# Hybrid Conformer and differential-attention block on one core: the first norm's squares taken from the channel-major x

## The chip, the cores and the metric

The kernel runs on one core of one Trainium2 chip. The metric is the device time of one execution in microseconds (us); lower is better. PE is TensorE, the matrix engine; DVE, ACT and POOL are the vector, scalar and GpSimd engines; SP is SyncE, whose queue issues most transfers. "Group 0" below is the first pair of 256-column groups of the input projection, "group 1" the next 256 columns.

## The reference, cut to what matters

T = 256 tokens, D = 2048 channels, one layer, all in float32:

```python
h = rmsnorm(x, norm_mix_g)                       # x * rsqrt(mean(x^2) + 1e-6) * g
a, g, q, k, v = split(h @ w_in)                  # 2048 -> 1024+1024 | 1024 | 1024 | 1024
u = layernorm(causal_dwconv(a * sigmoid(g), width 31))
conv_out = silu(u)
attn_out = rmsnorm(diff_attention(q, k, v, lam)) * (1 - lambda_init)
x = x + concat(conv_out, attn_out) @ w_out
gate, up = split(rmsnorm(x, norm_ffn_g) @ w_up)  # 2048 -> 2 x 5632
x = x + (gelu(causal_dwconv(gate, width 3)) * up) @ w_down
return rmsnorm(x, norm_final_g)
```

## The kernel before

Every product is split: x and each weight are cut into a rounded part `hi` and a rest `lo`, and three products per 128 input channels (hi by x-hi, hi by x-lo, lo by x-hi) are summed in PSUM. ACT writes the weights' `hi` (`split`, L151), DVE subtracts to `lo` (L152); `hi` and `lo` have three buffers each, one holding 1024 columns. `split_rows` does the same for x times the norm's gain (ACT L113, DVE L114). The kernel has five stages: input projection with the first norm, attention and convolution woven in between groups, output projection, gated FFN, down projection with the final norm.

**Start.** x comes channel-major as `xt` and is read with the weights in pieces of one or two blocks of 128 channels (`XPARTS`). The first `SIDE` pieces of x are issued by ACT (L258), everything else by SP through `fetch` (L139), in the order in which the code is written; SP first issues the gain `mix_g`. `WARM` matmuls on a tile of ones (L240, two PE passes each) run ahead of the first product. Group 0 multiplies block by block as the pieces arrive (L283) into four PSUM tiles `first`: two for the 256 columns of `a`, two for the 256 columns of `g`. The pool `acc` has just these four buffers. The next 256 columns of `a` (`early`) are loaded behind it in pieces of 8, 4 and 4 blocks.

**First norm.** The factor 1/rms of each token (`rstd1`) is not multiplied into x but into the products. Its squares come from a token-major copy `x_sb`, four loads of 512 KB among those of `early`: ACT squares with a running sum (L295), DVE adds the four parts (L298), POOL raises to the power -1/2 (`rsqrt_of`, L95, L96), and `spread` makes a row of it: DVE scales an identity (L102), PE multiplies it by ones (L103), DVE copies the result out as `rb1` (L104).

**Turn from group 0 to group 1.** As soon as group 0 is summed, `first` is copied out of PSUM, which needs no `rb1`, and multiplied later:

```python
if j == 0:
    with prio(ATT):
        nc.scalar.copy(a_, pa[n])
nc.vector.tensor_tensor(a_, a_ if j == 0 else pa[n], rb1, op=ALU.mult)
```

(L374 and L375; the same for `g_` on DVE, L382 and L383.) `channel_group` (L208 to L210) then takes two of the `acc` buffers per 256 columns.

**Order.** SP, ACT and DVE each run their instructions in a fixed order. SP's is that of the code; that of ACT and DVE comes from a scheduler that sorts by priority (`prio`); PE's is by hand from the group loop on. Small steps of attention and LayerNorm sit in a list `bg`; every fourth block of a group runs one of them (`tick`). At the end of the input projection the list holds `seq(ln_total, ln_mean, turn), value, None, ln_var, put, ln_apply`: the LayerNorm's sum over channels (L555), its mean by a matmul (L560), differences and squares (L566 to L574), and the variance by `token_sums` (two 128x1 products L109, copy L110), `rsqrt_of` and `spread`.

**Tail.** The last 512 columns of the down projection end token half by token half; the second half is cut in two parts of 256 columns. Of the last part DVE adds the residual (L708), ACT squares it with a sum (L710), POOL adds the sum to the earlier ones and takes the power (L718, L719), then DVE and ACT scale four pieces of 512 columns (L724 to L728), each stored by SP (L729).

## Time and profile before

| what | value |
| --- | --- |
| median of three runs | 1089.92 us (1089.47 to 1090.38) |
| the profiled execution: own time, span | 1090.31 us, 1088.5 us |
| PE busy | 1077.5 us, 99% of the span |
| DVE busy, ACT busy, POOL busy | 764.9 us, 599.1 us, 15.3 us |
| moved by DMA | 205.89 MB, mean 189 GB/s |

The span lies 1.8 us inside the profiled execution's own time, and that time lies 0.39 us above the median. "Busy" counts instructions as the profile shows them. A row of the timeline gives the start, the length (of all the instructions on the row together), the engine, the source line, the operation with destination and source, and how many there are; in brackets stands how long the engine idled before and what ended the wait. Lengths of instructions on one engine overlap by some hundredths of a microsecond, so the pace is read from starts.

### The profile page before, as it was taken

Reading aid. Unit: us, or ns where it says so; the run is one execution under the profiler, and the core shown is the slowest. Engines: PE = TensorE matmul, PEld = TensorE weight load, DVE = VectorE, ACT = ScalarE, POOL = GpSimd, SP = SyncE. Lnnn points to the kernel's source line nnn. Section 1 sums busy time; section 2 is a strip of 40 time slices with the busy share of each in tenths; the row PEclk is TensorE's granted clock in tenths of the full one; section 3 lists DMA queues with packets and bytes.
Section 4 is the critical chain, followed back from the end, with each engine's and each line's share of the span. In section 5 each row is a group of like instructions: output and inputs, shape, how many; then the busy total and the mean of one; then the engine's idle time right before and its main releaser. Section 6 shows DMA issues by size and latency. Waiting matters only on the chain.

```text
span 1088.5 us, 16124 instructions
## 1 busy us (share of the span) xinstructions
PE 1077.5 (99%) x6311; PEld 951.5 (87%) x6311; DVE 764.9 (70%) x1202; ACT 599.1 (55%) x973; POOL 15.3 (1%) x44
## 2 busy tenths in 40 slices
PE   9999999999999999999999999999999999999996
PEld 9999999998888888888888888888888888888885
DVE  6799999988765777776777677776777445454544
ACT  6776889886755454545445444544545434343432
POOL 0000000001000000000000000000000000000000
PEclk9999999999999999999999999999999999999998
DMA  9755544444555555555555555555555655555553
GB/s 352 244 192 185 190 165 152 155 163 148 201 178 178 186 194 192 184 183 181 193 191 193 194 187 180 184 189 189 194 193 190 231 192 196 192 194 193 195 166 107
DMA packets 32844, 205.89 MB, mean 189 GB/s; under 512 B 3712, under 2 KB 4480, under 8 KB 9600
## 3 DMA queue, kind: packets, MB, share of 16 engines
q1 hardware_dynamic: 32336, 203.55, 54.2%
q8 instruction: 49, 0.80, 0.3%
q0 software_dynamic: 144, 1.05, 0.2%
q10 hardware_dynamic: 288, 0.26, 0.1%
q14 instruction: 27, 0.22, 0.1%
HBM read 202.75 MB, written 2.10 MB: 188 GB/s over the span
## 4 chain that ended last, share of the span: by engine, by line
PE 97%; DMA 1%; DVE 1%; ACT 0%; issue 0%; POOL 0%; POOLq 0%; DVEq 0%; SPq 0%; ACTq 0%
PE acc L187 30%; PE acc L190 15%; PE acc L218 11%; PE acc L220 11%; PE acc L219 11%; PE acc L208 5%; PE acc L210 5%; PE acc L209 5%; PE acc L283 2%; DMA v_sb<-in_w_in 1%; PE misc L629 0%; PE misc L426 0%; PE misc L423 0%; PE misc L454 0%; DVE lo L152 0%; ACT hi L151 0%
## 5 line engine op out<-in xcount | busy, mean ns | idle before, releaser
L152 DVE TENSOR_TENSOR lo<-raw,hi 128x1024 fp32r<-128x1024 f32 x368 | 450.0, 1223 | 270.0 <-ACT hi L151 268.7
L151 ACT CAST hi<-raw 128x1024 fp32r<-128x1024 f32 x368 | 386.6, 1051 | 389.3 <-PE acc L220 171.5
L187 PE MATMUL acc<-actT,hi 128*128 128x512 f32 x1408 | 481.7, 395 | 0.0
L190 PE MATMUL acc<-actT,lo 128*128 128x256 f32 x1408 | 368.8, 280 | 0.0
L187 PEld LDWEIGHTS acc<-actT,hi 128*128 128x128 f32 x1408 | 253.3, 188 | 48.5
L190 PEld LDWEIGHTS acc<-actT,lo 128*128 128x128 f32 x1408 | 265.4, 188 | 13.7
L219 PE MATMUL acc<-lo,fT 128*128 128x512 f32 (+1 forms) x355 | 137.5, 387 | 0.0
L220 PE MATMUL acc<-hi,fT 128*128 128x512 f32 (+1 forms) x355 | 137.5, 387 | 0.0
L208 PE MATMUL acc<-actT,hi 128*128 128x256 f32 x448 | 127.6, 285 | 0.0
L210 PE MATMUL acc<-actT,lo 128*128 128x256 f32 x448 | 127.0, 283 | 0.2 <-DVE lo L152 0.2
L209 PE MATMUL acc<-actT,hi 128*128 128x256 f32 x448 | 126.8, 283 | 0.0
L218 PE MATMUL acc<-hi,fT 128*128 128x512 f32 (+1 forms) x355 | 123.8, 387 | 0.0
L208 PEld LDWEIGHTS acc<-actT,hi 128*128 128x128 f32 x448 | 85.9, 192 | 0.7 <-issue 0.7
L210 PEld LDWEIGHTS acc<-actT,lo 128*128 128x128 f32 x448 | 85.9, 192 | 0.4 <-DVE lo L152 0.4
L209 PEld LDWEIGHTS acc<-actT,hi 128*128 128x128 f32 x448 | 85.9, 192 | 0.0
L220 PEld LDWEIGHTS acc<-hi,fT 128*128 128x128 f32 x355 | 66.7, 188 | 13.7
L219 PEld LDWEIGHTS acc<-lo,fT 128*128 128x128 f32 x355 | 66.7, 188 | 13.6
L218 PEld LDWEIGHTS acc<-hi,fT 128*128 128x128 f32 x355 | 66.7, 188 | 13.5
L345 ACT ACTIVATE tap<-u,cols 128x256 f32<-128x256 f32 x160 | 71.0, 503 | 3.7 <-DVE cv L346 2.0
L234 ACT COPY half<-acc 128x256 f32<-128x256 f32 x88 | 32.4, 368 | 56.9 <-PE acc L187 56.9
L346 DVE TENSOR_TENSOR cv<-cv,tap 128x512 f32<-128x512 f32 x80 | 54.7, 685 | 3.0 <-ACT tap L345 1.2
L219 PE MATMUL acc<-lo,mixT 128*128 128x512 f32 x128 | 50.2, 392 | 0.0
(180 smaller groups left out, 913.6 us busy)
## 6 DMA issues: line engine op xcount, KB each, us to landing
raw<-in_w_up SPq DMA_DIRECT2D x88, 1024.0 KB, 4.9
raw<-in_w_down SPq DMA_DIRECT2D x43, 1024.0 KB, 4.9
raw<-in_w_in SPq DMA_DIRECT2D x35, 1024.0 KB, 4.9
raw<-in_w_out SPq DMA_DIRECT2D x14, 1024.0 KB, 4.9
mixT<-in_w_in SPq DMA_DIRECT2D x4, 512.0 KB, 8.4
x_sb<-in_x SPq DMA_DIRECT2D x4, 512.0 KB, 11.0
raw<-in_w_out SPq DMA_DIRECT2D x4, 512.0 KB, 3.5
out<-x_sb SPq DMA_DIRECT2D x8, 256.0 KB, 2.9
```

The lines of the kernel that those rows point to most:

```text
L151: cast(hi, src)
L152: nc.vector.tensor_tensor(lo, src, hi.bitcast(F32), op=ALU.subtract)
L187: nc.tensor.matmul(ps[n], lhsT=hi[:, cs], rhs=xT[:, k], start=(k == 0), stop=last)
L190: nc.tensor.matmul(ps[n][:, 1, :], lhsT=lo[:, cs], rhs=xT[:, k, 0, :], start=False, stop=last)
L208: nc.tensor.matmul(ps[n], lhsT=hi[:, cs], rhs=xT[:, k, 0, :], start=(k == 0), stop=False)
L209: nc.tensor.matmul(ps[n], lhsT=hi[:, cs], rhs=xT[:, k, 1, :], start=False, stop=False)
L210: nc.tensor.matmul(ps[n], lhsT=lo[:, cs], rhs=xT[:, k, 0, :], start=False, stop=(k == KD - 1))
L218: nc.tensor.matmul(ps, lhsT=xT[:, k, 0, ts_], rhs=hi, start=(k == first), stop=False)
L219: nc.tensor.matmul(ps, lhsT=xT[:, k, 0, ts_], rhs=lo, start=False, stop=False)
L220: nc.tensor.matmul(ps, lhsT=xT[:, k, 1, ts_], rhs=hi, start=False, stop=(k == last))
L345: nc.scalar.activation(tmp[:, n, :], upad[c][:, k : k + T], AF.Copy, scale=cwcol(k, c))
L346: nc.vector.tensor_tensor(cv[j], cv[j], tmp, op=ALU.add)
```

## The change

Squares of the first norm are now taken from the channel-major pieces: ACT squares each piece (L272), DVE adds the squares up (L275, L294), and `token_sums` adds them over channels. The `x_sb` loads move into the loop over the query groups, one each; `early` is loaded in two pieces of 8 blocks with the parameters between them. ACT issues only piece 0 of x, and `mix_g` behind it; SP starts with the first weights. Four one-block pieces become six, ten warm-ups eight. Group 0's copies go: `rb1` is multiplied straight from PSUM (L372, L378). The list at the end of the input projection is `turn, seq(ln_total, ln_mean, value), None, None, seq(ln_var, put), ln_apply`. In the tail DVE squares with a running sum (`last_part`), POOL takes only the power, and the second token half is stored in five pieces of 256 to 512 columns over the queues of SP and ACT.

```diff
     AHEAD = -200
-    XPARTS = [1, 1, 1, 1, 2, 2, 2, 2, 2, 2]
-    WARM = 10
-    SIDE = 2
+    XPARTS = [1, 1, 1, 1, 1, 1, 2, 2, 2, 2, 2]
+    WARM = 8
+    SIDE = 1
     ATT = -300
     HALF = 1024
...
-        ss1 = const.tile([P, NT, D // XW], F32, name="ss1")
+        sq1 = p1.tile([P, 2, T], F32, name=f"cv{CC // GW - 1}")
...
                 nc.scalar.dma_start(xraw[:, k0 : k0 + nk, :], xt[:, k0 : k0 + nk, :])
+                nc.scalar.dma_start(mix_g, norm_mix)
             pieces.append((k0, nk, raw, spans))
...
-            if i == 0:
-                fetch(mix_g, norm_mix)
...
                 split_rows(xT[:, k, 0, :], xT[:, k, 1, :], xraw[:, k, :], mix_g[:, k : k + 1])
+            h0 = k0 % 2
+            sqs = p2.tile([P, 2, T], F32, name="tap") if i > 1 else sq1
+            sq = sqs[:, h0 : h0 + nk, :]
+            nc.scalar.activation(sq, xraw[:, k0 : k0 + nk, :], AF.Square)
+            if i > 1:
+                total = sq1[:, h0 : h0 + nk, :]
+                nc.vector.tensor_tensor(total, total, sq, op=ALU.add)
             cast = nc.vector.tensor_copy if i == 0 else nc.scalar.copy
...
-        early = load(wi, 0, 8, GW, GW)
-        for i in range(D // XW):
-            if i == 2:
-                early.extend(load(wi, 8, 4, GW, GW))
-            cs = slice(i * XW, (i + 1) * XW)
-            fetch(x_sb[:, :, cs], xv[:, :, cs])
-            for t in range(NT):
-                junk = misc.tile([P, 512], F32, name="misc")
-                nc.scalar.activation(junk, x_sb[:, t, cs], AF.Square, accum_out=ss1[:, t, i : i + 1])
-        early.extend(load(wi, 12, 4, GW, GW))
         with prio(ATT):
-            nc.vector.tensor_reduce(rstd1, ss1, axis=AX.X, op=ALU.add)
+            nc.vector.tensor_tensor(sq1[:, 0, :], sq1[:, 0, :], sq1[:, 1, :], op=ALU.add)
+            token_sums(rstd1, sq1[:, 0, :])
             rsqrt_of(rstd1, rstd1, D, NORM_EPS, NT)
             spread(rb1, rstd1)
+        early = load(wi, 0, 8, GW, GW)
         load_params()
+        early.extend(load(wi, 8, 8, GW, GW))
...
             for n in range(2):
                 a_ = p2.tile([P, T], F32, name=f"a{n}")
-                if j == 0:
-                    with prio(ATT):
-                        nc.scalar.copy(a_, pa[n])
-                nc.vector.tensor_tensor(a_, a_ if j == 0 else pa[n], rb1, op=ALU.mult)
+                with prio(ATT if j == 0 else 0):
+                    nc.vector.tensor_tensor(a_, pa[n], rb1, op=ALU.mult)
                 an.append(a_)
             pg = first[2:] if j == 0 else channel_group(wi, CC + j * GW, xT, n_conv=RATE_A)
             for n in range(2):
                 g_ = p2.tile([P, T], F32, name="g_")
-                if j == 0:
-                    with prio(ATT):
-                        nc.vector.tensor_copy(g_, pg[n])
-                nc.vector.tensor_tensor(g_, g_ if j == 0 else pg[n], rb1, op=ALU.mult)
+                with prio(ATT if j == 0 else 0):
+                    nc.vector.tensor_tensor(g_, pg[n], rb1, op=ALU.mult)
                 gn.append(g_)
             for n in range(2):
...
+            cs = slice(j * XW, (j + 1) * XW)
+            fetch(x_sb[:, :, cs], xv[:, :, cs])
             pq = channel_group(wi, 2 * CC + j * GW, xT, n_conv=RATE_Q)
...
-        bg.extend([seq(ln_total, ln_mean, turn), value, None, ln_var, put, ln_apply])
+        bg.extend([turn, seq(ln_total, ln_mean, value), None, None, seq(ln_var, put), ln_apply])
...
-        STORES = (("dve", 0, 512), ("act", 512, 1024), ("dve", 1024, 1536), ("dve", 1536, 2048))
+        STORES = {
+            0: ((nc.vector, nc.sync, 512), (nc.scalar, nc.sync, 512), (nc.vector, nc.sync, 512), (nc.vector, nc.sync, 512)),
+            1: (
+                (nc.vector, nc.sync, 256), (nc.scalar, nc.scalar, 384), (nc.vector, nc.sync, 512),
+                (nc.vector, nc.sync, 448), (nc.vector, nc.scalar, 448),
+            ),
+        }
...
-        def finish(t, ss):
+        def last_part(t, ps, cs, before):
+            xs = x_sb[:, t, cs]
+            nc.vector.tensor_tensor(xs, ps, xs, op=ALU.add)
+            sums = const.tile([P, 1], F32, name=f"sums{t}_{cs.start}")
+            junk = misc.tile([P, 512], F32, name="misc")
+            nc.vector.tensor_tensor_reduce(
+                out=junk[:, : cs.stop - cs.start], in0=xs, in1=xs, scale=1.0 / D, scalar=before,
+                op0=ALU.mult, op1=ALU.add, accum_out=sums,
+            )
+            return sums
+
+        def finish(t, sums, cs):
             r3 = rstd3[:, t : t + 1]
-            for part in ss:
-                nc.gpsimd.tensor_tensor(r3, part, r3, op=ALU.add)
-            nc.gpsimd.tensor_tensor(r3, r3, mhalf[:, 0:1], op=ALU.pow)
-            c0 = D - XW
-            for eng, lo_, hi_ in STORES:
...
+            nc.gpsimd.tensor_tensor(r3, sums, mhalf[:, 0:1], op=ALU.pow)
+            lo_ = 0
+            for eng, queue, width in STORES[t]:
+                xs = x_sb[:, t, lo_ : lo_ + width]
+                cut = min(max(cs.start - lo_, 0), width)
+                if cut < width:
+                    xg = xs[:, cut:]
+                    nc.vector.scalar_tensor_tensor(xg, xg, r3, gf[:, lo_ + cut : lo_ + width], op0=ALU.mult, op1=ALU.mult)
+                if not cut:
+                    pass
+                elif eng is nc.scalar:
+                    nc.scalar.activation(xs[:, :cut], xs[:, :cut], AF.Copy, scale=r3)
                 else:
-                    nc.vector.tensor_scalar_mul(xs, xs, r3)
-                nc.sync.dma_start(ov[:, t, lo_:hi_], xs)
+                    nc.vector.tensor_scalar_mul(xs[:, :cut], xs[:, :cut], r3)
+                queue.dma_start(ov[:, t, lo_ : lo_ + width], xs)
+                lo_ += width
...
+            whole = slice(c0, D)
+            finish(0, last_part(0, pd[0], whole, rstd3[:, 0:1]), whole)
...
-            ss4 = const.tile([P, 2], F32, name="ss4")
...
-            residual(1, pd[1][:, left], slice(c0, c0 + hw), ss4[:, 0:1])
+            sums = last_part(1, pd[1][:, left], slice(c0, c0 + hw), rstd3[:, 1:2])
...
+            xl = x_sb[:, 1, c0 : c0 + hw]
...
-            residual(1, tail, slice(c0 + hw, D), ss4[:, 1:2])
-            finish(1, [ss4[:, 0:1], ss4[:, 1:2]])
+            sums = last_part(1, tail, slice(c0 + hw, D), sums)
+            nc.vector.tensor_tensor(xl, xl, gf[:, c0 : c0 + hw], op=ALU.mult)
+            finish(1, sums, slice(c0 + hw, D))
```

PE's order at the turn from group 0 to group 1, before (L283 is group 0, L208 to L210 group 1, L103 the `spread` of `rb1`):

```order
L283 MATMUL acc<-actT,hi 128x256 x2
L283 MATMUL acc<-actT,lo 128x256
L208 MATMUL acc<-actT,hi 128x256 [waits Activation_49]
L209 MATMUL acc<-actT,hi 128x256
L210 MATMUL acc<-actT,lo 128x256 [waits DVE_49]
```

and with the change (L289 is group 0 now, L109 the sums over channels, `cv_105` the buffer of squares):

```order
L289 MATMUL acc<-actT,hi 128x256 x2
L289 MATMUL acc<-actT,lo 128x256
L109 MATMUL misc<-ones,cv_105 128x1 [waits DVE_49]
L109 MATMUL misc<-ones,cv_105 128x1
L103 MATMUL misc<-diag,ones 128x128 [waits DVE_49] x2
L208 MATMUL acc<-actT,hi 128x256 [waits DVE_49,Activation_49]
L209 MATMUL acc<-actT,hi 128x256
```

The sums and `spread` moved from inside group 1 to a place between the groups, and the first product of group 1 waits for DVE as well as ACT.

DVE's order at the same place with the change (`raw`, `hi` and `lo` are the early weights, `nlam` the attention's lambda):

```order
L152 TENSOR_TENSOR lo<-raw,hi 128x1024 [waits PE_49,Activation_49]
L309 TENSOR_TENSOR nlam<-ls 128x1 [waits Activation_49]
L110 COPY rstd_104<-misc 128x2 [waits PE_49]
L310 TENSOR_SCALAR nlam<-nlam 128x1 [waits DVE_49]
L152 TENSOR_TENSOR lo<-raw,hi 128x1024 [waits DMAHW2_49,Activation_49]
L102 TENSOR_SCALAR diag<-ident,rstd_104 128x128 [waits Pool_49]
L102 TENSOR_SCALAR diag<-ident,rstd_104 128x128
L314 TENSOR_SCALAR nrq_482<-rstd_104 128x2
L104 COPY rb_106<-misc 128x256 [waits PE_49]
L372 TENSOR_TENSOR a_502<-acc,rb_106 128x256 [waits DVE_49]
L372 TENSOR_TENSOR a_504<-acc,rb_106 128x256
```

The third `lo` of the early weights stands between the copy of the sums (L110) and the scaled identity (L102), and the multiplication out of PSUM (L372) stands where the copies used to be.

ACT's order at the start, with the change (L258 and L259 are its transfers of piece 0 and `mix_g`, L272 the squares of pieces 0 and 1, L113 the split of x):

```order
L258 DMA mixT<-in_xt 128x256
L259 DMA mix_g<-in_norm_mix 128x16
L262 ACT_TABLE_LOAD
L262 ACTIVATE touch<-mhalf 128x8 [waits Pool_49]
L272 ACTIVATE cv_105<-mixT 128x256 [waits DMAHW0_49]
L272 ACTIVATE cv_105<-mixT 128x256 [waits DMAHW2_49]
L113 ACTIVATE actT<-mixT,mix_g 128x256 [waits DMAHW3_49]
L113 ACTIVATE actT<-mixT,mix_g 128x256
```

Both squares stand ahead of the first split of x, and the second waits for piece 1 of x; before, the split was ACT's first work on x.

## Rows read from the trace of the kernel before

**Rows 1.** Page part 1, the whole span: engine, busy us, share, instructions.

```profile
PE 1077.5 (99%) x6311; PEld 951.5 (87%) x6311; DVE 764.9 (70%) x1202; ACT 599.1 (55%) x973; POOL 15.3 (1%) x44
```

**Rows 2.** Page part 4, the chain that ended last: share by engine.

```profile
PE 97%; DMA 1%; DVE 1%; ACT 0%; issue 0%; POOL 0%; POOLq 0%; DVEq 0%; SPq 0%; ACTq 0%
```

**Rows 3.** Timeline of PE, 0 to 15 us (columns as described above).

```profile
0.98 4.64 PE L240 MATMUL misc<-ones 128*128 128x128 f32 x20 [0.98 <-POOL ones L86]
5.27 2.01 PE L283 MATMUL acc<-actT,hi 128*128 128x256 f32 x8
...
7.59 1.12 PE L283 MATMUL acc<-actT,hi 128*128 128x256 f32 x8
...
12.23 1.22 PE L283 MATMUL acc<-actT,hi 128*128 128x256 f32 x8 [0.17 <-ACT hi L151]
...
14.06 1.12 PE L283 MATMUL acc<-actT,hi 128*128 128x256 f32 x8
```

**Rows 4.** Windows: us, busy PE PEld DVE ACT POOL, granted clock, DMA share, GB/s.

```profile
5.00:7.00 2.00, 2.00 (x11) 2.00 (x11) 1.84 (x4) 1.56 (x4) 0.00 (x0) 1.00 1.03 363
...
40.00:50.00 10.00, 9.76 (x81) 9.55 (x81) 9.90 (x18) 7.32 (x12) 0.00 (x0) 1.00 0.54 173
```

**Rows 5.** Timeline of SP's queue, DVE and ACT, 1 to 5 us.

```profile
1.17 0.90 SPq L139 DMA_DIRECT2D v_sb<-in_w_in  x2
...
4.46 0.43 DVE L151 CAST hi<-v_sb 128x512 fp32r<-128x512 f32 x1 [0.39 <-DMA v_sb<-in_w_in]
...
4.71 0.51 ACT L113 ACTIVATE actT<-mixT,mix_g 128x256 fp32r<-128x256 f32 x1 [1.14 <-DMA mixT<-in_xt]
```

**Rows 6.** Timeline of DVE, 16 to 19 us, in group 0.

```profile
16.13 1.22 DVE L152 TENSOR_TENSOR lo<-mixT,hi 128x1024 fp32r<-128x1024 f32 x1
...
18.08 1.22 DVE L152 TENSOR_TENSOR lo<-mixT,hi 128x1024 fp32r<-128x1024 f32 x1
```

**Rows 7.** Timeline of ACT and PE at the turn, 28.9 to 31 us.

```profile
28.93 0.62 ACT L374 COPY a<-acc 128x256 f32<-128x256 f32 x2
...
29.91 0.28 PE L208 MATMUL acc<-actT,hi 128*128 128x256 f32 x1
...
30.69 1.04 ACT L151 CAST hi<-raw 128x1024 fp32r<-128x1024 f32 x1
```

**Rows 8.** Timeline of PE and DVE, 38.7 to 42.6 us, in group 1.

```profile
38.78 0.61 PE L103 MATMUL misc<-diag,ones 128*128 128x128 f32 x4
...
39.43 0.42 DVE L104 COPY rb<-misc 128x256 f32<-128x256 f32 x1 [1.58 <-PE misc L103]
...
39.89 0.76 DVE L375 TENSOR_TENSOR a<-a,rb 128x256 f32<-128x256 f32 x2
...
42.51 0.39 PE L210 MATMUL acc<-actT,lo 128*128 128x256 f32 x1 [0.24 <-DVE lo L152]
```

**Rows 9.** Timeline of PE, DVE and POOL, 255 to 269 us, the LayerNorm.

```profile
255.13 0.70 PE L560 MATMUL misc<-part,onesc 128*128 128x256 f32 x2 [0.69 <-DVE part L555]
...
263.01 0.43 DVE L574 TENSOR_TENSOR part<-u 128x256 f32<-128x256 f32 x1
...
265.89 0.50 PE L109 MATMUL misc<-ones,part 128*128 128x1 f32 x4
...
266.95 0.70 POOL L96 TENSOR_TENSOR rln<-rln,mhalf 128x2 f32<-128x2 f32 x1
...
268.31 0.47 DVE L102 TENSOR_SCALAR diag<-ident,rln 128x128 f32<-128x128 f32 x2
```

**Rows 10.** Timeline of DVE, ACT and POOL, 1080 to 1082.2 us, the tail.

```profile
1080.21 0.42 DVE L708 TENSOR_TENSOR x_sb<-acc,x_sb 128x256 f32<-128x256 f32 x1
...
1080.67 0.39 ACT L710 ACTIVATE misc<-x_sb 128x256 f32<-128x256 f32 x1 [0.35 <-DVE x_sb L708]
...
1081.59 0.55 POOL L719 TENSOR_TENSOR rstd<-rstd,mhalf 128x1 f32<-128x1 f32 x1
```

**Rows 11.** Page part 6, transfers: count, KB each, median us from issue to landing.

```profile
out<-x_sb SPq DMA_DIRECT2D x8, 256.0 KB, 2.9
```

More of the change, by code (lines that the diff above doesn't have):

```diff
@@ L713, in residual @@
             )
-        def finish(t, ss):
-            r3 = rstd3[:, t : t + 1]
-            for part in ss:
-                nc.gpsimd.tensor_tensor(r3, part, r3, op=ALU.add)
-            nc.gpsimd.tensor_tensor(r3, r3, mhalf[:, 0:1], op=ALU.pow)
-            c0 = D - XW
-            for eng, lo_, hi_ in STORES:
-                xs = x_sb[:, t, lo_:hi_]
-                if hi_ == D:
-                    nc.vector.scalar_tensor_tensor(xs, xs, r3, gf[:, c0:], op0=ALU.mult, op1=ALU.mult)
-                elif eng == "act":
-                    nc.scalar.activation(xs, xs, AF.Copy, scale=r3)
-                else:
-                    nc.vector.tensor_scalar_mul(xs, xs, r3)
-                nc.sync.dma_start(ov[:, t, lo_:hi_], xs)
+        def last_part(t, ps, cs, before):
[9 more added lines that the diff above has]
+        def finish(t, sums, cs):
+            r3 = rstd3[:, t : t + 1]
+            nc.gpsimd.tensor_tensor(r3, sums, mhalf[:, 0:1], op=ALU.pow)
[10 more added lines that the diff above has]
+                    nc.scalar.activation(xs[:, :cut], xs[:, :cut], AF.Copy, scale=r3)
+                else:
+                    nc.vector.tensor_scalar_mul(xs[:, :cut], xs[:, :cut], r3)
+                queue.dma_start(ov[:, t, lo_ : lo_ + width], xs)
+                lo_ += width
         def plain_end(s, pd):
@@ L754, in block_kernel @@
             token_step(pd[0], rest, 0, fT, 0, NF - 1)
-            residual(0, pd[0], slice(c0, D), ss3[:, 0, s : s + 1])
-            finish(0, [ss3[:, 0, s : s + 1]])
+            whole = slice(c0, D)
+            finish(0, last_part(0, pd[0], whole, rstd3[:, 0:1]), whole)
             token_step(pd[1], rest[:-CUT], 1, fT, 0, NF - 1)
-            ss4 = const.tile([P, 2], F32, name="ss4")
             hw = XW // 2
```

## The prediction, made before the changed kernel had run

> **What bounds the kernel now.** I read the shares of busy time first, then the chain of waits, then the timelines of the places that the change touches. PE is busy for 1077.5 of 1088.5 us [rows 1] and holds 97% of the chain that ended last [rows 2]; DVE at 70% and ACT at 55% stand beside it. So a microsecond counts only if PE loses or regains it, or if it lies behind PE's last product. The reader is to see in the timelines where PE is not at its pace. At the start its products come at half of it: the first eight of group 0 take 2.01 us, the next eight hi products 1.12 [rows 3]. In group 0 it waits for pieces of weights near 12 us, in group 1 once for DVE's `lo` at 42.5 us [rows 8], and before the LayerNorm's mean for DVE's sum [rows 9]. Everything else between 7 and 1079 us runs at one product of 256 columns per 0.12 us. The change has about 2 us of such waits to win, and some 3 us at the tail to shorten a little.
>
> All sums are made on the profiled execution, own time 1090.31 us, 0.39 above the median of 1089.92.
>
> **First product, +0.2 (-0.1 to +0.7).** Today it starts at 5.27, when the 20 passes of the warm-ups, (5.27 - 0.98) / 20 = 0.2145 each, are done [rows 3]. Sixteen passes end at 0.98 + 16 x 0.2145 = 4.41. But ACT's new order has the squares of pieces 0 and 1 ahead of the first split of x, and piece 1 is now SP's second transfer. Today it is ACT's second, and ACT takes it up at 4.71 [rows 5]. On SP it stands one issue slot of 0.45 us (0.90 for two, [rows 5]) behind the weights, which leave one slot earlier than today, so I expect it near 4.5. Then comes a square of 128x256 (0.39 in the tail's row [rows 10]; with the step to the next 0.45) and the split, 0.51 [rows 5]: about 5.5. Early end: piece 1 at 4.2, so 5.2. Late end: piece 1 at 4.7 and full lengths, some 5.7, and 6.0 if `mix_g`, now behind x on ACT's queue, is late too. The eight slow products stay slow in either case.
>
> **Waits for pieces in group 0, -0.7 (-0.7 to 0).** Blocks 1 to 3 take 3 x 1.44 us from 7.59, so block 4 could start at 11.91; it starts at 12.23, and its twelve products last until 14.06 where 1.44 would do [rows 3]: 0.32 + 0.39 lost, while ACT casts a piece of two blocks that came whole. With six single blocks the cast of block 4 takes half as long and waits for half the bytes, so the loss should go. It stays if the transfers are late for another reason. The squares are new work in group 0, per two blocks one square and one DVE sum of 128x512. DVE's pace today is 18.08 - 16.13 = 1.95 us per two blocks [rows 6]; with some 0.7 for the sum it is 2.65, under PE's 2.88. Cost there: nothing, with 0.2 us of cover.
>
> **Turn from group 0 to group 1, +3.85 (+3.2 to +4.4).** Today ACT copies the `a` sums out at 28.93 and group 1 starts at 29.91 with no gap [rows 7]; the norm's chain runs beside group 1, `spread` interrupts PE at 38.78 for four passes of 0.11, 0.45 in all [rows 8]. Now the four PSUM buffers come free only by the multiplication by `rb1`, and the whole chain lies between the groups on PE's own queue. Let T be the end of group 0:
> - Sums over channels, copy and power: in the LayerNorm the same steps run from 265.89 to 266.95 + 0.70 = 267.65, so T + 1.76 [rows 9].
> - DVE cannot scale the identity then. The third early `lo` stands ahead of it and needs ACT's cast of a buffer that group 0's last products free: the cast takes 1.04 [rows 7], the `lo` 1.22 [rows 6], so DVE is at it until T + 2.35.
> - One scaled identity, 0.47 / 2 [rows 9]: T + 2.6.
> - PE's matmul to DVE's copy, 39.43 - 38.78 = 0.65; the copy to the multiplication, 39.89 - 39.43 = 0.46; one multiplication, 0.42 [rows 8]: T + 4.13. With the step to PE group 1 starts at T + 4.2, and its first products run some 0.1 slower, as after the wait at 42.5.
>
> That is 4.3, less the 0.45 which `spread` costs today: 3.85. If the scheduler's `lo` were out of the way, the chain alone gives 1.76 + 0.25 + 0.65 + 0.46 + 0.42 + 0.1, less 0.45: 3.2. If ACT's cast is half a microsecond late, 4.4. The copies that go were hidden and bring nothing. The weights of group 1 are there (SP has no `x_sb` ahead of them), so nothing else is late behind it.
>
> The rule that speaks against this edit is in the Trainium skill, Perfetto Trace Analysis, Matmuls: independent matmul groups should rotate through PSUM banks, so that one's evacuation overlaps the next one's products. By that rule kept, as today, the term would be about -0.45 and the sum -1.6; by the new order the rotation is gone.
>
> **Wait at 42.5 us, -0.4 (-0.5 to 0).** PE idles until DVE's `lo` arrives, behind the four multiplications at 39.89 [rows 8]. They move to the turn, so this goes unless DVE's backlog only shifts.
>
> **LayerNorm's order, -0.25 (-0.85 to +0.3).** `turn` ahead of `ln_mean` gives DVE time for its sum; the wait at 255.13 (0.69 idle, 0.85 with the slower restart) goes [rows 9]. In return mean and variance are two empty steps apart plus `value`, three steps in all. The chain between them ran from 255.13 to 263.01 + 0.43, 8.3 us [rows 9]; beside one more `lo` and cast it is 10.5. The three steps from the mean to the sums take 265.89 - 255.13 = 10.8 today [rows 9], less what `value` brought, some 10. About 0.6 of new wait is the middle, and none or 1.15 the ends.
>
> **x_sb in the query groups, 0.** Four loads of 512 KB go to stretches in which DMA is about half busy (0.54, [rows 4]). They cost an issue slot of 0.45 each on SP ahead of weights that are loaded two buffers early. If that cover is gone, 512 KB at the 363 GB/s of [rows 4] is 1.4 us once, part of the upper end of the last term.
>
> **Tail, -0.2 (-0.6 to +0.3).** From ACT's square at 1080.67 to the power at 1081.59 lie 0.92 us [rows 10]. DVE's square with sum lasts about as long as the residual's 0.42 [rows 10], with the step to POOL 0.55: the power starts 0.35 earlier. But the end is a stream of 1 MB; one store takes 2.9 us to land [rows 11], and narrower pieces on two queues shift only when it begins. I take half.
>
> **DVE without slack, +0.2 (0 to +0.8).** From 40 to 50 us DVE is busy 9.90 of 10 [rows 4]. PE and DVE both stand still at the turn, and what DVE defers (taps, `lo`) it has no room to make up there; one wait like that at 42.5 may come back.
>
> Sum: 0.2 - 0.7 + 3.85 - 0.4 - 0.25 - 0.2 + 0.2 = +2.7. 1090.31 + 2.7 = 1093.0, less 0.39: **1092.6 us**. The ends that go together leave 1091 to 1093.8 for this case alone.
>
> **The rivals.**
> - **A, the clock.** There are now a hole of 1 us between warm-ups and products and one of 4.2 us at the turn. The granted clock prints 1.00 for 5 to 7 us [rows 4], but the products there come every 0.213 us, 256 columns at 1.2 GHz, and after 7.1 us every 0.12; before that PE had been working since 0.98 [rows 3]. If PE comes back at the lower level after a hole and keeps it as long as at the start, 6.1 us, it loses 0.44 of each: 2.7. For it: the holes are longer than any that PE has today once it is up. Against it: after the wait at 42.5 only one product was slow. In the middle 1.9, so 1094.5 (1093.4 to 1095.3). The Trainium skill says, in TensorE: Matmul & The Clock Gate, Part 1, that "the default state is throttled, and activity releases the throttle"; no stretch of this trace shows a fall.
> - **B, the other side: group 1 is not held by `rb1`.** If its first products find a free buffer, or the chain is done by T because the sums run ahead of the last blocks, the term of 3.85 is about 0, and 1088.7 is left; with the first product at 4.5 and no new LayerNorm wait 1087.2. It decides where T + 4.2 falls below T. Against it: PE's written order has the sums behind group 0's last product and the wait for DVE on group 1's first.
> - **C, the first product comes early.** If piece 1 lands by 3.5, the warm-ups' end at 4.41 is the limit, 0.95 better than the forecast: 1091.7. For it: nothing but `mix_g` and x are ahead of the weights now. Against it: ACT could take piece 1 up at 4.71 today [rows 5].
>
> **How the numbers follow.** A measurement of this kernel tells about 0.2%, 2.2 us, from no change: slower begins at 1092.1, faster at 1087.7. The forecast has 0.62: 0.40 above 1092.1, 0.21 within, 0.01 faster. A has 0.18, all slower. B has 0.10: 0.06 the same, 0.04 faster. C has 0.10: 0.08 the same, 0.02 slower. That makes 0.60 slower, 0.35 the same, 0.05 faster. The range of 1090.6 to 1095.2 takes in the forecast but for its far ends, C and nearly all of A, and leaves B out.
>
> **What would show it.** PE's timeline should have a hole of about 4 us between L289 and L208, broken by L109 and L103, with L372 as what ends it; no wait near 12 and 42 us; a first product near 5.5 behind ACT's split; a short wait ahead of the LayerNorm's L109 and none ahead of L560. The forecast is wrong if group 1 starts within 1 us of group 0's end, if the hole is over 5 us, if products of 0.21 us follow it, or if DVE's lost time returns as waits over 1 us before 100 us.

## The result, and the profile after

| | median | range | runs | profiled execution: own time, span |
| --- | --- | --- | --- | --- |
| before | 1089.84 us | 1089.47 to 1090.38 | 6 | 1090.31, 1088.5 us |
| changed | 1096.66 us | 1095.79 to 1097.08 | 6 | 1095.86, 1093.8 us |

The ratio is 1.0062, with a 95% interval of 1.0051 to 1.0073: 6.8 us slower. That is the forecast's side but past its range (up to 1095.2). The changed kernel's executions spread over 1.3 us, and the profiled one lies 0.8 below their median. One execution of a later kernel (e9) took 2171.16 us, twice as long as all others, and is left out of every figure here.

The shares of the whole span hardly moved (page parts 1 and 4; against [rows 1, 2]):

```profile
PE 1079.0 (99%) x6311; PEld 952.8 (87%) x6311; DVE 772.1 (71%) x1220; ACT 596.7 (55%) x961; POOL 15.3 (1%) x41
```

```profile
PE 96%; DVE 2%; issue 1%; ACT 1%; DMA 0%; POOLq 0%; POOL 0%; DVEq 0%; ACTq 0%
```

The places are found in the timelines again. PE at the start (columns as before: start, length, engine, line, what, how many, wait):

```profile
0.98 3.78 PE L240 MATMUL misc<-ones 128*128 128x128 f32 x16 [0.98 <-POOL ones L86]
6.10 1.26 PE L289 MATMUL acc<-actT,hi 128*128 128x256 f32 x8 [1.34 <-ACT actT L113]
...
7.68 1.12 PE L289 MATMUL acc<-actT,hi 128*128 128x256 f32 x8
```

The first product comes at 6.10, behind 1.34 us of idle PE, but its eight take 1.26 and not 2.01 [rows 3]: the clock was up already. Block 1 begins at 7.68 against 7.59, there is no wait near 12 us, and group 0's last product begins at 29.26 instead of 29.79. What held the first product stands in ACT's rows and, for transfers of the first 3 us, in the transfer view (count, KB each, median us from issue to landing):

```profile
4.93 0.72 ACT L272 ACTIVATE cv<-mixT 128x256 f32<-128x256 f32 x2 [1.78 <-DMA mixT<-in_xt]
...
5.56 0.89 ACT L113 ACTIVATE actT<-mixT,mix_g 128x256 fp32r<-128x256 f32 x2
```

```profile
mixT<-in_xt ACTq DMA_DIRECT2D x1, 128.0 KB, 4.2
mix_g<-in_norm_mix ACTq DMA_DIRECT2D x1, 8.0 KB, 4.2
```

In the kernel before the same view reads

```profile
mixT<-in_xt ACTq DMA_DIRECT2D x2, 128.0 KB, 2.9
...
mix_g<-in_norm_mix SPq DMA_DIRECT2D x1, 8.0 KB, 2.1
```

so it was not piece 1 that came late: the very first piece of x, issued at 0.72 in both, landed at 4.9 instead of 3.0, beside the 256 KB of weights that SP now issues first. Not all of the 1.9 us comes with that order: in seven later profiles that have it too, the piece landed at 4.0 to 4.2. The other 0.8 shows only in this profile and in that of e4, and its cause is open.

The turn, PE with DVE and POOL:

```profile
29.38 0.51 PE L109 MATMUL misc<-ones,cv 128*128 128x1 f32 x4
...
30.45 0.72 POOL L96 TENSOR_TENSOR rstd<-rstd,mhalf 128x2 f32<-128x2 f32 x1
...
30.58 1.23 DVE L152 TENSOR_TENSOR lo<-raw,hi 128x1024 fp32r<-128x1024 f32 x1 [0.44 <-ACT hi L151]
31.72 0.48 DVE L102 TENSOR_SCALAR diag<-ident,rstd 128x128 f32<-128x128 f32 x2
32.06 0.81 PE L103 MATMUL misc<-diag,ones 128*128 128x128 f32 x4 [2.17 <-DVE diag L102]
...
32.91 0.42 DVE L104 COPY rb<-misc 128x256 f32<-128x256 f32 x1 [0.63 <-PE misc L103]
33.37 0.75 DVE L372 TENSOR_TENSOR a<-acc,rb 128x256 f32<-128x256 f32 x2
...
33.94 0.55 PE L208 MATMUL acc<-actT,hi 128*128 128x256 f32 x1 [1.07 <-DVE a L372]
```

From the end of group 0 at 29.38 to group 1's first product at 33.94 lie 4.56 us, where there were 0 [rows 7]. And then the clock (windows: us, busy PE PEld DVE ACT POOL, granted clock, DMA share, GB/s):

```profile
28.00:34.00 6.00, 2.76 (x22) 2.41 (x21) 4.22 (x12) 2.53 (x3) 0.92 (x2) 0.88 0.68 251
34.00:39.20 5.20, 5.20 (x25) 5.20 (x25) 4.46 (x11) 3.36 (x8) 0.00 (x0) 0.50 0.03 6
39.20:44.00 4.80, 4.80 (x41) 4.80 (x41) 4.10 (x6) 4.44 (x8) 0.00 (x0) 0.98 0.32 73
```

From 34.0 to 39.2 PE is busy all the time at a granted clock of 0.50: 25 products, one per 0.213 us, where 5.2 us hold 43. Summed over the starts from L208's first on, 2.46 us go there. The wait at 42.5 [rows 8] is gone. At the LayerNorm the mean now meets no wait, the sums do, 1.00 us over the usual step (before: 0.85 at the mean [rows 9]):

```profile
273.88 0.42 DVE L571 TENSOR_TENSOR part<-u 128x256 f32<-128x256 f32 x1
274.45 0.58 PE L109 MATMUL misc<-ones,part 128*128 128x1 f32 x4 [0.84 <-DVE part L571]
```

And the tail:

```profile
1085.17 0.28 PE L220 MATMUL acc<-hi,fT 128*128 128x256 f32 x1
...
1086.74 0.49 DVE L723 CUSTOM_DVE_ANT_0 misc<-x_sb,sums 128x256 f32<-128x256 f32 x1
...
1087.36 0.56 POOL L731 TENSOR_TENSOR rstd<-sums,mhalf 128x1 f32<-128x1 f32 x1 [3.85 <-DVE sums L723]
```

PE's last product ends at 1085.45, 5.80 later than before, and the span ends 8.35 behind it instead of 8.85. So of the two profiled executions: group 0's end -0.53, hole 4.56 less the 0.45 of the old `spread` = +4.11, clock +2.46, wait at 42.5 -0.5, LayerNorm +0.15, small waits of DVE +0.1, tail -0.5: +5.3, the difference of the spans.

### The profile page after: what moved, and what is told of

Its sections match the earlier page's. It is cut to its first block, busy times and chain, and to the rows that moved or that the text cites. A ratio compares the mean times of both kernels' runs of the same rounds, so it can differ in the third digit from the quotient of the medians.

```text
span 1093.8 us, 16131 instructions
## 1 busy us (share of the span) xinstructions
PE 1079.0 (99%) x6311; PEld 952.8 (87%) x6311; DVE 772.1 (71%) x1220; ACT 596.7 (55%) x961; POOL 15.3 (1%) x41
## 4 chain that ended last, share of the span: by engine, by line
PE 96%; DVE 2%; issue 1%; ACT 1%; DMA 0%; POOLq 0%; POOL 0%; DVEq 0%; ACTq 0%
PE acc L187 30%; PE acc L190 15%; PE acc L218 11%; PE acc L219 11%; PE acc L220 11%; PE acc L208 5%; PE acc L209 4%; PE acc L210 4%; PE acc L289 2%; DVE lo L152 1%; DMA mixT<-in_xt 0%; PE misc L626 0%; DVE pr L426 0%; PE misc L421 0%; DVE cv L345 0%
## 5 line engine op out<-in xcount | busy, mean ns | idle before, releaser
L208 PE MATMUL acc<-actT,hi 128*128 128x256 f32 x448 | 128.9, 288 | 1.1 <-DVE a L372 1.1
L210 PE MATMUL acc<-actT,lo 128*128 128x256 f32 x448 | 127.8, 285 | 0.0
L208 PEld LDWEIGHTS acc<-actT,hi 128*128 128x128 f32 x448 | 87.1, 194 | 2.0 <-issue 2.0
L210 PEld LDWEIGHTS acc<-actT,lo 128*128 128x128 f32 x448 | 87.0, 194 | 0.0
```

What stands on the lines that cost most here:

```text
L208: nc.tensor.matmul(ps[n], lhsT=hi[:, cs], rhs=xT[:, k, 0, :], start=(k == 0), stop=False)
L210: nc.tensor.matmul(ps[n], lhsT=lo[:, cs], rhs=xT[:, k, 0, :], start=False, stop=(k == KD - 1))
```

## The experiments

Each time stands against the kernel before on the same chip (medians 1089.62 to 1089.68 in all sessions); "below the changed kernel" is against its 1096.66. **Theory 1**: group 1 is held because the buffers of group 0 come free only by `rb1`, and the clock falls through that hole. Its rivals are in the expectations.

**e1_copies**, group 0's copies put back (those of `a`; those of `g_` likewise):

```diff
-                with prio(ATT if j == 0 else 0):
-                    nc.vector.tensor_tensor(a_, pa[n], rb1, op=ALU.mult)
+                if j == 0:
+                    with prio(ATT):
+                        nc.scalar.copy(a_, pa[n])
+                nc.vector.tensor_tensor(a_, a_ if j == 0 else pa[n], rb1, op=ALU.mult)
```

> The changed kernel with group 0's four copies out of PSUM put back (multiplied by rb1 later). Theory 1 (the buffers: group 1 waits for rb1 only because the four buffers of group 0 are freed by the multiplication, and the clock falls because of that hole): group 1 starts within 0.7 us of group 0's end, no stretch at granted clock 0.50, 6.0 us less than the changed kernel, about 1089.5 to 1090.6. Theory 2 (the place of the sums and of spread on PE's queue is what holds group 1, the buffers come free late as well): the hole of 4.5 us shrinks to about 2.9 and the clock still falls, about 1095. Theory 3 (the clock falls for another reason, fewer warm-ups or the narrow sums): no hole, but products at 0.21 us after the turn all the same, about 1092.5.

Measured: 1091.45 us (1089.89 to 1091.93), 5.2 below the changed kernel. Group 1 follows the sums at once, and the clock stays up:

```profile
29.67 0.50 PE L109 MATMUL misc<-ones,cv 128*128 128x1 f32 x4
30.03 0.36 PE L208 MATMUL acc<-actT,hi 128*128 128x256 f32 x1
```

```profile
34.00:39.20 5.20, 5.20 (x46) 5.20 (x46) 4.22 (x8) 2.96 (x5) 0.00 (x0) 1.00 0.57 191
```

The sums still stand between the groups and cost 0.36, so they are not what held group 1, and theory 3 falls. `spread` now stands inside group 1, so e1 does not part its place on PE's queue from the held buffers; but while group 1's first product needs a buffer that only `rb1` frees, `spread` has to run ahead of it. The time is 0.85 above the expected upper end and spreads over 2 us.

**e2_fill**, matmuls on the tile of ones in the hole:

```diff
             rsqrt_of(rstd1, rstd1, D, NORM_EPS, NT)
-            spread(rb1, rstd1)
...
+            dummy(10)
+            pb = misc.tile([P, 512], F32, name="misc")
+            for t in range(NT):
...
+            nc.vector.tensor_copy(rb1, pb[:, :T])
+            dummy(5)
```

(`dummy(n)` is n matmuls on the tile of ones, `spread` is written out between them, and every one of these matmuls is tied behind the one before.)

> The changed kernel with 15 further matmuls on the tile of ones in the hole (ten between the sums and spread, five behind spread), nothing else. If the idle PE is what brings the clock down (theory 1), group 1's start stays at 4.5 us behind group 0's end, but its products come every 0.12 us: 2.4 us less than the changed kernel, about 1094.2. If the clock falls for another reason (theory 3), the products stay at 0.21 us and the time stays at 1096.7. If the added matmuls delay spread, up to 0.5 us of that is given back.

Measured: 1095.46 us (1095.17 to 1096.83). PE at the start, at the turn with POOL, and once in the attention, then a window behind the turn; the profiled execution took 1096.47:

```profile
5.32 2.07 PE L289 MATMUL acc<-actT,hi 128*128 128x256 f32 x8 [0.56 <-ACT actT L113]
...
8.05 1.80 PE L289 MATMUL acc<-actT,hi 128*128 128x256 f32 x8
...
30.90 2.25 PE L301 MATMUL misc<-ones 128*128 128x128 f32 x18
...
31.60 1.72 POOL L96 TENSOR_TENSOR rstd<-rstd,mhalf 128x2 f32<-128x2 f32 x1
...
33.70 0.71 PE L310 MATMUL misc<-diag,ones 128*128 128x128 f32 x4 [0.54 <-DVE diag L309]
34.24 1.28 PE L301 MATMUL misc<-ones 128*128 128x128 f32 x10
...
35.47 0.36 PE L208 MATMUL acc<-actT,hi 128*128 128x256 f32 x1
...
166.79 0.84 PE L466 MATMUL misc<-ident,pr 128*128 128x128 f32 x3 [0.63 <-DVE pr L457]
```

```profile
34.00:39.20 5.20, 5.20 (x45) 5.09 (x44) 4.09 (x11) 2.97 (x7) 0.00 (x0) 1.00 0.00 2
```

With PE at work in the hole the granted clock stays at 1.00: the fall is the hole's doing. The stretch between the groups stays (30.31 to 35.47) and is 0.6 longer: one of the added matmuls runs ahead of the sums (0.22), and POOL's power, which `spread` waits for, shows 1.72 us instead of 0.72; why is open. As a price of the clock the time is not clean. The median fell by 1.2 of the expected 2.4, and part of that is chance: three of the five executions are of the shorter kind here (1095.17 to 1095.46), two of six in the changed kernel. Between the two profiled executions the rows give: end of group 0 +0.93 (products at half pace from 5.32 until 9.4, in the changed kernel at full pace from 6.1 on), the longer stretch +0.6, the clock -2.46, and waits for DVE in the attention, near 166 and 194 us, +1.5 (1.8 us against 0.3). That is +0.6, as the two times have it (1096.47 and 1095.86).

**e3_early**, no copies, but the chain earlier:

```diff
+            if i == len(pieces) - 1:
+                with prio(ATT):
+                    nc.vector.tensor_tensor(sq1[:, 0, :], sq1[:, 0, :], sq1[:, 1, :], op=ALU.add)
+                    sums_mm, sums_got = token_sums(rstd1, sq1[:, 0, :])
+                    rsqrt_of(rstd1, rstd1, D, NORM_EPS, NT)
...
+                    if last and i_ == 18:
+                        with prio(ATT):
+                            spread_mm, rb_got = spread(rb1, rstd1, prod)
```

> The changed kernel, group 0 still multiplied straight out of PSUM, but the chain put earlier: the sums over channels run ahead of the last two blocks' products, spread ahead of the last six products, and the early weights' first two lo's behind the sums' copy and behind the a multiplications. Theory 1a (it is the latency of the chain behind group 0 that costs, not the missing copies as such): rb1 is ready near group 0's end, the hole is under 0.8 us, no fall of the clock, 5.0 to 6.0 us less than the changed kernel, about 1091. If the multiplication out of PSUM costs by itself, the hole stays over 2 us and the clock falls: 1094 or more.

Measured: 1092.43 us (1091.08 to 1092.99), 4.2 below the changed kernel and not the 5 to 6 expected. The hole is 0.5 us, 30.57 to 31.08, and there is no fall of the clock; `spread` costs a wait of its own:

```profile
29.30 0.71 PE L103 MATMUL misc<-diag,ones 128*128 128x128 f32 x4 [0.33 <-DVE diag L102]
...
31.08 0.36 PE L215 MATMUL acc<-actT,hi 128*128 128x256 f32 x1 [0.36 <-DVE a L388]
```

So it is the chain behind the last product that costs. Multiplying straight out of PSUM, with the two waits shown, leaves 1.0 us over e1.

**e4_repeat**, the changed kernel again:

> The changed kernel unchanged, for the spread of its runs: two of six lay at 1095.8 and four near 1096.9. If how long the clock stays down after the hole differs from run to run, this profile shows a low stretch of another length than 5.4 us, or the same one at the same total; if the first transfers' landing differs (first piece at 4.9 us against 3.0 before), the first product starts at another time than 6.10.

Measured: 1096.78 us (1095.89 to 1097.61). The profile is again one of the shorter executions (1095.89). Its hole is 0.4 longer (29.59 to 34.55), since here all four passes of `spread` run at half pace, 1.22 us against 0.81 in the first profile:

```profile
32.26 1.22 PE L103 MATMUL misc<-diag,ones 128*128 128x128 f32 x4 [2.17 <-DVE diag L102]
```

The low stretch behind it ends sooner, at 38.7 instead of 39.4, and costs 1.9 instead of 2.46; hole and slow products together are 6.8 against 7.0. The spread was not explained by it.

**e5_start_back** and **e6_warm10** start from e1_copies:

```diff
# e5_start_back
-    XPARTS = [1, 1, 1, 1, 1, 1, 2, 2, 2, 2, 2]
-    WARM = 8
-    SIDE = 1
+    XPARTS = [1, 1, 1, 1, 2, 2, 2, 2, 2, 2]
+    WARM = 10
+    SIDE = 2
-                nc.scalar.dma_start(mix_g, norm_mix)
+            if i == 0:
+                fetch(mix_g, norm_mix)
# e6_warm10
-    WARM = 8
+    WARM = 10
```

> e1_copies with the start of the kernel before put back (gain first on SP, pieces 0 and 1 of x on ACT, four single blocks, ten warm-ups). Theory S1 (the start of the change costs: the weights as SP's first transfer let nothing land before 3.5 us, and the hole between the warm-ups' end at 4.8 us and the first product makes the clock's rise fall late in part of the executions): x's first piece lands near 3.0, the first product is at 5.3, no execution loses more than the 0.8 us that the kernel before loses, and the median falls from 1091.45 to about 1090.4. Theory S2 (the start of the change is no worse, what e1 loses against the kernel before is the sums on PE and a new wait near 161 us): the median stays at 1091.4 or rises by up to 0.3 because two-block pieces come back.

> e1_copies with ten warm-ups instead of eight, so that PE works until 5.27 us. Theory S1 (the hole of 0.5 us and more behind the warm-ups lets the clock's rise come late in part of the executions): the executions of 1091.5 to 1091.9 go, those of 1089.9 to 1090.5 stay, median about 1090.5. Theory S2 (the spread has nothing to do with the hole): the same spread, median 1091.4.

Measured: e5 1089.18 us (1088.77 to 1090.11), ratio to the kernel before 0.9997 (0.9989 to 1.0006); e6 1090.04 us, ten of eleven executions between 1089.71 and 1090.29. Both went S1's way, e5 1.2 further than expected. e5 takes back the copies and the start alone and stands level with the kernel before, so the loss lies in these two. Two more warm-ups are worth 1.4 us in the median, the rest of the start 0.86; in e5 the first piece of x landed at 2.95 again. The profiles of e5 and e6 don't show these 0.86 at the start: e6 ends group 0 at 29.04, e5 at 29.71, but e6 waits 0.93 near 160 us for DVE in the attention, and e5 does not. The order that the scheduler makes of DVE's work differs between the two.

**e7_tail** and **e8_ln**, the kernel before with one part of the change each:

> The kernel before with the change's tail alone. My forecast for it was -0.2 (-0.6 to +0.3); the trace of the changed kernel shows the time from PE's last product to the end of the span at 8.3 us against 8.9. Theory: -0.5, about 1089.1. Rival (the end is a stream of stores that DMA limits): within 0.2 of the kernel before.

> The kernel before with the change's LayerNorm order alone. Forecast -0.25 (-0.85 to +0.3); the trace of the changed kernel shows no wait ahead of the mean and 1.0 us of it ahead of the sums. Theory: the wait only moves, +0.15, about 1089.8, with PE idle for 1.0 us ahead of the 128x1 products. Rival (in the changed kernel DVE was late from the turn): the wait ahead of the sums is under 0.5 here and the time falls by 0.4 or more.

Measured: e7 1089.33 us, ratio 0.9998 (0.9989 to 1.0007); e8 1089.69 us, ratio 1.0001 (0.9992 to 1.0010). The tail's 0.5 shows in the rows (0.65 in e7's) and is too small for the interval. e8's waits (line, what for: us in total, times, longest) name the sums:

```profile
PE misc L109 <- DVE part L574: 0.8, 1, 0.8
```

The wait moved, as expected, and nothing was won.

**e9_combined** and **e10_before_ln_tail**, a later step for the sums, in e5 and in the kernel before with the new tail (the line that is put in):

```diff
+        bg.extend([turn, seq(ln_total, ln_mean, value), None, None, None, seq(ln_var, put), ln_apply])
```

> e5_start_back (copies and start as before, squares from the channel-major x, tail of the change) with one more empty step between the LayerNorm's mean and its sums. The wait of 1.0 us ahead of the 128x1 products should go, since one step of the output projection is some 3 us: 1.0 less than e5_start_back, about 1088.2, and 0.1% less than the kernel before. Rival: the normalised channels then come too late for the output projection and the wait turns up there: 1089.2 or more.

> The kernel before with the change's tail and with the LayerNorm order of e9_combined, squares and start as before. If the gains of e9_combined come from tail and LayerNorm alone, -0.85 - 0.4 = about 1088.4, the same as e9_combined within 0.4; if the channel-major squares bring something by themselves (no x_sb loads ahead of early weights, no wait near 42 us), e9_combined is 0.4 or more below this one.

Measured: 1093.69 us (1092.01 to 1094.38) and 1094.27 us (1092.71 to 1094.33): e9 on its rival's side and worse than its figure, e10 far above its 1088.4, with waits in the same place. PE in e9 now waits for what the LayerNorm hands to the output projection:

```profile
271.16 0.50 PE L218 MATMUL acc<-hi,mixT 128*128 128x512 f32 x1 [0.89 <-ACT mixT L113]
...
272.88 0.80 PE L220 MATMUL acc<-hi,mixT 128*128 128x512 f32 x1 [0.99 <-DVE mixT L114]
...
280.71 0.50 PE L218 MATMUL acc<-hi,mixT 128*128 128x512 f32 x1 [0.66 <-ACT mixT L595]
...
282.11 0.50 PE L220 MATMUL acc<-hi,mixT 128*128 128x512 f32 x1 [0.67 <-DVE mixT L596]
```

Behind the first two of these waits, 0.89 and 0.99 us, the clock falls here too, and PE is busy at half of it (a window, columns as above):

```profile
273.40:275.80 2.40, 2.40 (x7) 1.84 (x6) 0.00 (x0) 0.00 (x0) 0.00 (x0) 0.50 0.12 51
```

What the channel-major squares are worth by themselves is not shown: e9 and e10 overlap, and e5 and e7, which differ by more than the squares, lie 0.15 apart.

**e11_warm4**, e1_copies with four warm-ups:

> e1_copies with four warm-ups, so that PE idles from 2.7 to 5.3 us. Theory S1 (PE has to be at work without a hole before the clock rises; no profile so far shows a rise earlier than 4.2 us after PE's start or after such a hole): products at 0.21 us until 9 us or later, 1.6 to 2.7 us lost, median 1092 to 1093, 2 to 3 above e6_warm10. Theory S2 (warm-ups do not matter): 1091.4 as e1_copies.

Measured: 1090.55 us (1089.94 to 1091.21): the time went neither theory's way, the clock went S1's. The products run at half pace from 5.33 to 9.8, and group 1 begins 1.5 later than in e6. But this order of DVE's work has no wait near 160 us, which gives 0.93 back; half a microsecond is left, which is what was measured against e6. S1's figure of 4.2 us was read wrongly: in e8's profile, taken before, the passes of the warm-ups go over from one per 0.21 to one per 0.11 us at about 4.1 on the timeline, where 4.2 us behind PE's start would be 5.2.

**e12_fill_warm10**, e2_fill with ten warm-ups:

> e2_fill with ten warm-ups: both holes that touch the clock are closed, the wait for rb1 itself stays. Expected e2_fill's 1095.46 less the 1.4 us between e1_copies and e6_warm10: about 1094.1, that is some 4 us above e6_warm10, all of it in the 4.2 to 4.6 us between group 0's last product and group 1's first. If the clock still falls at the turn: 1096.

Measured: 1095.04 us, no low stretch at the turn. Group 0 ends at 29.12, group 1 begins at 34.28, 5.16 us in between as in e2. The waits in the attention, near 165 and 193 us, are e2's too, 1.8 us in both, so they are not what the time lies 0.9 above the expected by. The expectation took 1.4 us of late rise off e2's median, and that was one of e2's shorter executions already. Between the profiled ones, e2's with the late rise and this one, lie 1.2 us (1096.47 and 1095.26), and that is where group 0 ends: 30.31 and 29.12.

**e13_after_warm10**, the changed kernel with ten warm-ups only:

> The changed kernel with ten warm-ups instead of eight, nothing else. Theory S1 (in most executions the hole behind the warm-ups lets the clock rise late): the upper executions of 1096.5 to 1097.6 go, those near 1095.8 stay, median 1095.3 to 1095.8, 1 us below the changed kernel. Theory S2 (the spread comes from the turn, where the clock falls for longer in some executions): the median stays at 1096.7.

Measured: 1095.62 us (1095.37 to 1096.16). The executions above 1096.2 are gone, S1's way, and the median is 1.0 us lower. Part of that is not the clock: the two profiled executions differ by 0.5 (1095.86 and 1095.37) with the products at full pace from the first in both, since here the first piece of x landed at 4.1, the first product came at 5.39, and group 0 ended at 28.91. That the longer executions lost the rest to a late rise of the clock is argued: with eight warm-ups, the profiles of shorter executions (the changed kernel, e1, e3, e4) show the clock up at the first product, and the only one of a longer execution (e2) does not.

**e14_ln_mean** and **e15_ln_mean_parts**, e5 with the mean behind the transposes, and six single blocks in e15:

```diff
-        bg.extend([turn, seq(ln_total, ln_mean, value), None, None, seq(ln_var, put), ln_apply])
+        bg.extend([seq(ln_total, turn, ln_mean), value, None, ln_var, put, ln_apply])
```

> e5_start_back with the LayerNorm's steps where the kernel before has them, but the mean's matmul behind turn's transposes within the first step. The transposes cover some 0.7 of the 0.85 us that PE waits for DVE there, and the sums keep the place where the kernel before does not wait: neither wait over 0.3 us, 0.7 to 1.0 less than e5_start_back, about 1088.3. Rival: the mean is then late for the sums three steps on, and the 1.0 us stays ahead of the 128x1 products: 1089.2.

> e14_ln_mean with the change's six single blocks. They take away the wait of 1.0 us near 11 to 13 us that e5_start_back shows (e6_warm10, with six single blocks, ends group 0 0.67 earlier): 0.5 less than e14_ln_mean, about 1087.8. Rival: group 0 ends earlier but DVE's work after it does not, and waits in the attention (0.9 us near 161 in e6_warm10) give it back: no difference.

Measured: e14 1088.37 us (1087.76 to 1088.91), ratio 0.9986 (0.9978 to 0.9995): some 1.3 us below the kernel before, a small gain whose interval stays below 1. Neither mean nor sums wait there:

```profile
254.35 0.60 PE L562 MATMUL misc<-part,onesc 128*128 128x256 f32 x2
```

e15: 1088.77 us, ratio 0.9993 (0.9984 to 1.0002). The waits near 11 and 13 us go, one of 0.93 us near 159 comes, as its rival said; in the median there is no gain over e14.

## Why the prediction was right and wrong

**The turn: right.** The term was 3.85 (3.2 to 4.4); it measured 4.56 - 0.45 = 4.11 (4.5 in e4 and e13, where `spread` ran at half pace throughout). Step by step behind T = 29.38: the power ends at +1.79 (forecast 1.76), DVE's `lo` at +2.43 (2.35), `spread` starts at +2.68 (2.6), DVE's copy at +3.53 (3.25, since the clock was down already), group 1 at +4.56 (4.2). e1 and e3 show both conditions, held buffers and a chain behind the last product.

The Trainium skill's rule (Perfetto Trace Analysis, Matmuls: rotate PSUM banks, so that evacuation overlaps the next group's products) is what this edit gave up; e1 against the changed kernel, 5.2 us, agrees with it.

**The clock: the step that failed.** The forecast's sum gave PE its full pace back behind the hole, and put the loss into rival A, 0.18, with 1.9 us and 1094.5. The clock fell in all three profiles with PE idle in that hole, and the slow products cost 2.46 (1.9 in e4, 2.05 in e13). So rival A's size was near, and the forecast's own sign of being wrong, products of 0.21 us behind the hole, came; what failed is that the sum had nothing for it. The argument against it was that after the wait at 42.5 only one product was slow [rows 8]; but PE idled 0.24 us there, and 2.17 and then 1.07 here. A short wait says nothing of a long one. e2 shows the cause by filling the hole.

The Trainium skill, TensorE: Matmul & The Clock Gate, Part 1, says that "the default state is throttled, and activity releases the throttle". The trace agrees, with 0.50 from 34.0 to 39.2 us behind the hole.

**The first product: the second step that failed.** "+0.2 (-0.1 to +0.7)", with piece 1 as what is late and "the eight slow products stay slow in either case". In the profiled execution it was 6.10, later than the late end of 6.0, because the first piece of x landed 1.9 us later; the slow products were gone there, and block 1 began only 0.1 later. So in the rows the term came out near its 0.2 by luck: two errors cancelled. In the median the start cost 2.3 (e1 against e5), of which 1.4 by the warm-ups (e6) that I had only counted for when they end. That PE idles for 0.5 us and more behind them, with the clock rising late in part of the executions, was missing from the sum, though rival A's words on "a hole of 1 us between warm-ups and products" named the place.

**The small terms.** Waits in group 0: -0.7 forecast, gone in the profile. Wait at 42.5: -0.4, gone. LayerNorm: -0.25 forecast, +0.15 in the rows and nothing measurable in e8; the middle of the new wait was 0.6 and it is 1.0. Tail: -0.2 forecast, -0.5 in the rows. DVE's lateness: +0.2 forecast, 0.1 in the rows. With the first product's 0.2 they were forecast at -1.15 together; the rows give 5.3 - 4.11 - 2.46 = -1.3.

So the rows account for 4.1 + 2.5 - 1.3 = 5.3 us; the medians differ by 1.5 more, since the changed kernel's profile lies 0.8 below its median and that of the kernel before 0.5 above, and the own times differ by 0.25 more than the spans. Two more warm-ups take 1.0 of it back (e13), not all by the clock. With 2.5 and 1.0 in it the forecast would have said 1096.1.

## What to carry to other kernels

Multiplying out of PSUM in place of copying saved nothing here, where the copies were beside PE's work, and it makes every buffer wait for the factor: follow the factor's chain from the last product that feeds it and put it ahead of the end, or keep the copy. A hole in PE's work is priced twice, by its length and by the products at half pace behind it (here 4.6 us of hole, 2.5 us of slow products). The second part came behind idle times of 2.17 and 1.07 us, and in e9 behind 0.89 and 0.99; it did not come behind 0.24 at 42.5 us or 0.69 at 255 us in the kernel before. Look for a row with a hole like the one in question. And a wait that is "moved to a later step" has to be followed to its consumer: the LayerNorm's 1 us could be hidden behind other PE work in the same step (e14), not by one more step (e9).

## What was not expected of the hardware

- The first transfers land later in the new order: with 8 KB of gain first on SP, x's first 128 KB landed at 2.9 to 3.3 us in the profiles; with 256 KB of weights first, at 4.0 to 4.9, though issued at 0.72 in both. The weights themselves, issued 0.44 earlier, landed at 3.8 to 4.7 instead of 4.4 to 4.9. The two starts differ in ACT's second transfer as well, and no run takes these apart.
- The clock's rise at the start varies by the execution: with ten warm-ups the products were at full pace by 5.0 to 7.1 us in the profiles. With eight it was up by 5.3 in e1 and e3, by 6.1 in the changed kernel, and only at 9.4 in e2. The length of the idle time behind the warm-ups does not order them: 0.56 us in e2, 1.34 in the changed kernel.
- A slower start need not cost its full price: against e1, e11 is 2.0 us behind in its third block, but begins group 1 only 0.84 later (30.87 and 30.03), since e1's faster PE loses 1.0 to late pieces near 14 to 16 us.
- One step in the scheduler's order of DVE moves 0.9 us of wait into or out of the attention (near 160 us in e1, e6 and e15, none in e5, e11 and e14; 1.8 us in e2 and e12) without any edit there. In e6 one more `lo` stands just ahead of what PE waits for. Which edit brings it stays open.
